# A decoder block's expert stage: a third of the weighted one-hot tiles moved to ScalarE, ten U chunks moved to the dense stage, six chunks' activations kept on chip

## The chip, the cores and the metric

One NeuronCore of a Trainium2 chip runs the whole program. The metric is device time in microseconds (us) of one execution, median of the runs shown. Engine names are those of the profile: PE is the matrix engine, PEld its weight load, DVE the vector engine, ACT the scalar engine, POOL the general engine, SP the engine that issues most DMAs.

## The reference

The program computes one decoder block for 512 tokens of width 1024: attention and gated linear attention, then a product-key expert layer (PEER) and a final norm. Everything the change touches lies in the expert layer. Per token it selects 128 of 16384 experts (8 heads, 16 each) with gates, and computes

```python
ub = jnp.take(u, eb, axis=0)
hid = jax.nn.gelu(jnp.einsum('tkd,td->tk', ub, xb), approximate=False) * gb
vb = jnp.take(v, eb, axis=0)
return jnp.einsum('tk,tkd->td', hid, vb)
```

`u` and `v` are 16384 x 1024 float32, 64 MiB each. `eb` holds the experts of a block of tokens, `gb` their gates.

## The kernel before

**Dense and gathered tokens.** The 512 tokens are four blocks of 128. Blocks 0, 1 and 2 (384 tokens) go the dense way: all experts are multiplied, and the gates of the experts not chosen are zero. Block 3 goes the gathered way: POOL fetches rows of `u` and `v` by index (`fetch_u` and `gather_u`, L1330 and L1340; `gather_v`, L1365 and L1370) and DVE does the dot products and sums. Of the dense blocks, the last 64 tokens get their U products by gathered rows too (`sp_gather` L1278, `sp_dot` L1284: 64 of them, called dots here), so a U product is 128 experts x 320 tokens.

**Chunks.** The experts are 128 chunks of 128, and four chunks `4m`..`4m+3` form one `m`. A chunk's U part is 24 matmuls of 320 columns (`u_matmuls`; `mm3`, L76 to L78, multiplies a high and a low part of each operand); ACT makes the high part of the weights (L69), DVE the low part (L70), and ACT the gelu (`u_gelu`, L965). The V part is 18 matmuls of 512 columns.

**U chunks ahead.** Ninety-six of the 128 U chunks (all even ones, and the odd ones of m = 16 to 31) are computed before the dense stage, list `AHEAD`. Two chunks share one 1 MiB load (`u_load`) and one result tile `ge` of three. When both are done, the ACT queue writes the tile to the DRAM buffer `gsp` (L980).

**The gate stage.** Gates of the dense blocks are made expert by token with one-hot products. For eight tokens (called a half group; two make one of 24 groups, so there are 48) DVE makes a tile `o12` by comparison (`one_hot`, L1178: 128x2048 bf16) one half group in advance, then a weighted tile `o2` (L1196: 128x3072 bf16), which is the second one-hot times the three bf16 parts of the gate. PE does 24 matmuls of 128 columns (L1203), and ACT evicts two PSUM banks (L1205). `o12` has five buffers, shared with other tiles, and `o2` three. The parts of the gate come from `gate_transposes`, `gate_parts` and `gate_rest`. The half groups of block 0 and the first ten of block 1 have two dots each, until the 64 are used up; the last 22 have none. The chunks ahead are placed between these pieces.

**The order of the work.** In this stage the order on DVE and POOL is that of the program (`manual_schedule`), while PE, ACT and SP are ordered by the framework's own timeline. Where the next U chunk goes is decided by two running sums: each piece yields its estimated DVE time and PE time, and a chunk is put in while `p * DVE_ALL < (d + LEAD_U) * PE_ALL`, at 1.14 of DVE and 3.52 of PE. A half group yields 1.14 and 1.68 of DVE and 1.4 of PE.

**The dense stage.** From here on PE, ACT and SP follow the program too. The list `xs` holds the work units: for each `m` one U unit (the two odd chunks, where they were not made ahead) and two V units of two chunks each: 16 U and 64 V units. A unit loads 1 MiB of `u` or `v` into a ring of four tiles (`load_x`, class `Ring`); ACT makes the high part (L1622), DVE the low part (L1631). A V unit also multiplies the stored activations with the gates (L1621) and splits the product (L1625, L1638). The activations come back from `gsp` by `load_pair`, into a ring `pairs` of five tiles: first the three old `ge` tiles, then two new ones. `loads(i)` decides in which order SP issues these loads, and asks for pairs first. Gates come from `Gd`, 1.5 MiB for eight chunks. The 252 remaining row gathers of block 3 are spread over the units by `due`.

Of the kernel before, what the change touches and what calls it, by code (L numbers as in the profile page):

```python
# [7 lines left out]
F32 = mybir.dt.float32  # L8
FR = mybir.dt.float32r
BF = mybir.dt.bfloat16  # L10
I32 = mybir.dt.int32
U32 = mybir.dt.uint32
AF = mybir.ActivationFunctionType
OP = mybir.AluOpType
# [3 lines left out]
P = 128  # L18
# [13 lines left out]
NGRP = TD // TG  # L32
# [4 lines left out]
SB = DENSE[-1]  # L37


ODD_AHEAD = tuple(range(16, 32))  # L40
AHEAD = tuple(c for m in range(P // 4) for c in (4 * m, 4 * m + 2) + ((4 * m + 1, 4 * m + 3) if m in ODD_AHEAD else ()))
RING, RING2 = 3, 2
GR, G2 = 5, 3
TCARGS = dict(schedule_with_timeline_sim=True)
# [3 lines left out]
def peer_block_kernel(ctx: ExitStack, tc: tile.TileContext, a: dict, out: bass.AP):  # L48
# [900 lines left out]
                nc.scalar.activation(h2n[:, half * 512:(half + 1) * 512], pb, AF.Copy)  # L949

    gsp = dr.tile([P // 2, P, 2, TU], F32, name="gsp")
    last_gelu = {}

    def u_load(c):
        u_part.raw[c % 2] = raw([P, 2, KD, P], f"u{c}")
# [8 lines left out]
    def u_gelu(dest, ph):  # L964
        last_gelu["u"] = nc.scalar.activation(dest, ph, AF.Gelu)  # L965

    def u_part(c, lo_eng=None, after=None):

        j = c // 2 % 2
        if j == 0:  # L970
            u_load(c)
            u_part.ge = dnA.tile([P, 2, TU], F32, tag="ge", bufs=RING, name=f"ge{c}")
        with tc.issue_after(gelus[-4].ins) if len(gelus) > 3 and lo_eng is None else nullcontext():
            uh, ul = hilo(u_part.raw[c % 2][:, j], [P, KD, P], f"uc{c}", lo_eng or nc.vector)
        with tc.issue_after(after.ins) if after is not None else nullcontext():
            ph, end = u_matmuls(c, uh, ul)
        u_gelu(u_part.ge[:, j], ph)
        gelus.append(last_gelu["u"])
        if j:
            nc.scalar.dma_start(gsp[c // 2 - 1:c // 2 + 1, :, c % 2, :].rearrange("j p t -> p j t"), u_part.ge)  # L980
        return end

# [137 lines left out]
    def gathered_index():  # L1120
        nc.vector.scalar_tensor_tensor(ix_u, I12[GB][:, 0], 128.0, I12[GB][:, 1], op0=OP.mult, op1=OP.add)
        odd = rt.tile([P, P], I32, name="odd")
        half = rt.tile([P, P], F32, tag="gr3", bufs=1, name="half")
        nc.vector.tensor_copy(odd, I12[GB][:, 1])
        nc.vector.tensor_scalar(odd, odd, 1, None, op0=OP.bitwise_and)
        nc.vector.tensor_copy(half, odd)
        nc.vector.scalar_tensor_tensor(half, half, -63.5, I12[GB][:, 0], op0=OP.mult, op1=OP.add)
        nc.vector.tensor_scalar(half, half, 2.0, None, op0=OP.mult)
        nc.vector.scalar_tensor_tensor(ix_v, I12[GB][:, 1], 128.0, half, op0=OP.mult, op1=OP.add)
        nc.vector.tensor_copy(gg_g, gates[GB])  # L1130
        yield 0.8, 0
# [10 lines left out]
    def gate_transposes(n):  # L1142

        t12 = rt.tile([P, P // 2, 2, 2], BF, tag="t12", bufs=2, name=f"t12{n}")
        for s in range(2):
            pt = bank(f"tr{s}{n}", BK[s])
            tr = nc.tensor.transpose(pt[:, :P], I12[n][:, s], ident)
            nc.scalar.activation(t12[:, :, s], pt[:, :P].rearrange("p (g r) -> p g r", r=2), AF.Copy)
        pt = bank(f"trg{n}", BK[2])
        nc.tensor.transpose(pt[:, :P], gates[n], ident)  # L1150
        gp3 = rt.tile([P, P // 2, 3, 2], BF, tag="gp3", bufs=2, name=f"gp3{n}")
        r = rt.tile([P, P], F32, tag="gr3", bufs=1, name=f"gr3{n}")
        pair = lambda v: v.rearrange("p (g r) -> p g r", r=2)
        nc.scalar.activation(gp3[:, :, 0], pair(pt[:, :P]), AF.Copy)
        trs[n] = t12, gp3, pt, r
        gate_transposes.tr = gate_transposes.tr or tr
        yield 0, 0.6
# [9 lines left out]
    def gate_rest(n):  # L1167
        gp3, pt, r = trs[n][1:]
        pair = lambda v: v.rearrange("p (g r) -> p g r", r=2)
        nc.vector.tensor_tensor(gp3[:, :, 2], pair(r), gp3[:, :, 1], OP.subtract)  # L1170
        yield 0.25, 0

    gate_transposes.tr = None
# [8 lines left out]
        return o12  # L1182

    def gate_group(bi, n, q):
        gp3 = trs[n][1]
        H = TB // 2
        if q % 2 == 0:
            gate_group.gs = rt.tile([P, P // CG, 2, CG, TG], F32, tag="gs", bufs=2, name=f"gs{n}{q}")
        gs = gate_group.gs
        for t0 in range(0, TG, TB):  # L1190
            g0 = (q * TG + t0) // 2
            o12 = gate_group.next or one_hot(n, g0)
            gate_group.next = one_hot(n, g0 + H) if g0 + H < P // 2 else None
            yield 1.14, 0
            o2 = rt.tile([P, H, 3, P, 2], BF, tag="o2", bufs=3, name=f"o2_{n}{q}{t0}")
            nc.vector.tensor_tensor(o2, o12[:, :, 1, None].to_broadcast([P, H, 3, P, 2]),  # L1196
                                    gp3[:, g0:g0 + H, :, None].to_broadcast([P, H, 3, P, 2]), OP.mult)
            for f in range(TB // 4):
                pt = bank(f"pg{n}{q}{t0}{f}", BK[f]).rearrange("p (a b) -> p a b", a=4)
                for i in range(4):  # L1200
                    g, r = divmod(4 * f + i, 2)
                    for m in range(3):
                        nc.tensor.matmul(pt[:, i, :], o12[:, g, 0, :, r], o2[:, g, m, :, r],  # L1203
                                         start=(m == 0), stop=(m == 2))
                evict = nc.scalar.activation(gs[:, :, q % 2, :, t0 + 4 * f:t0 + 4 * f + 4].rearrange("p c i a -> p a c i"),  # L1205
                                             pt.rearrange("p a (c i) -> p a c i", c=P // CG), AF.Copy)
            evicts.append(evict)
            yield 1.68, 1.4
        k = bi * (P // TG) + q
        if bi == len(DENSE) - 1:  # L1210
            nc.scalar.activation(gates_r[0][:, k], gs[:, 0, q % 2], AF.Copy)
        if q % 2:
            writes.append(lambda: (nc.gpsimd if k >= NGRP - 3 else nc.sync).dma_start(
                Gd[:, :, k - 1:k + 1].rearrange("c p g e -> p c (g e)"), gs.rearrange("p c g i t -> p c (g i t)")))
            if k != NGRP - 3:
                writes.pop()()
# [279 lines left out]
    work = chain(route_heads(), *head, woven(0, rows, first_block), woven(1, rows, second_block),  # L1496
                 woven(SB, [], third_block, gate_rest(SB)))
    NL_U = len(AHEAD) - LAST_U
    DVE_ALL = 11 + 4 * 7.6 + 3 + 1.15 * TS + 2.82 * 2 * NGRP + 1.15 * EARLY + 1.14 * (NL_U - WQ_U)
    PE_ALL = 1.4 * 2 * NGRP + 3 + UCOST * (NL_U - WQ_U)  # L1500
    ctx.enter_context(tc.manual_schedule(engines={mybir.EngineType.DVE, mybir.EngineType.Pool}))
    d = p = 0.0
# [60 lines left out]
    one_vraw = lambda name: dn.tile([P, 2, D], F32, tag="vraw", bufs=1, name=name)  # L1563
    old_ge = lambda name: dnA.tile([P, 2, TU], F32, tag="ge", bufs=RING, name=name)
    raws = Ring([one_raw] * 3 + [one_vraw])
    pairs = Ring([old_ge] * RING + [make_ge] * RING2)
    grs = Ring([lambda name: gk.tile([P, NGRP, CG, TG], F32, tag="gring", bufs=1, name=name), make_gr])
    xrest, prest, jrest = list(range(len(xs))), list(range(0, P, 2)), list(range(P // CG))
    src, ge = {}, {}

    def load_x():
        i = xrest.pop(0)
# [6 lines left out]

    def load_pair():  # L1580
        c = prest.pop(0)
        t = ge[c] = pairs.take(f"gp{c}", step["v", c])
        n = 1 if c // 4 in odd_here else 2
        nc.sync.dma_start(t[:, :n], gsp[c // 2, :, :n])

    def load_gates():
        j = jrest[0]
# [25 lines left out]
    def prep(i, extra=()):  # L1613
        k, c = xs[i]
        weigh()
        raw_ = src.pop(i)
        hi, lo = slots[i % 3]
        if k == "v":
            cs = c % CG
            A = gates_r[c // CG][:, :, cs:cs + 2, :]  # L1620
            nc.vector.tensor_tensor(A[:, :NGU], ge.pop(c).rearrange("p j (g t) -> p g j t", g=NGU), A[:, :NGU], OP.mult)  # L1621
        nc.scalar.activation(hi, raw_, AF.Copy)  # L1622
        if k == "v":
            Ah, Al = make_A(f"Ah{c}"), make_A(f"Al{c}")
            nc.scalar.activation(grp(Ah), A, AF.Copy)  # L1625
        before = due[i - 1] if i else EARLY
        if i > 1:
            gather_to((before + due[i] + 1) // 2)
        for piece in extra:
            piece()  # L1630
        nc.vector.tensor_tensor(lo, raw_, hi, OP.subtract)  # L1631
        gather_to(due[i])
        activate()
        if k == "u":
            ready[i] = [(h.rearrange("p (k e) -> p k e", k=KD), l.rearrange("p (k e) -> p k e", k=KD))
                        for h, l in ((hi[:, j], lo[:, j]) for j in range(2))]
        else:
            nc.vector.tensor_tensor(grp(Al), A, grp(Ah), OP.subtract)  # L1638
            ready[i] = [(c + j, Ah[:, j], Al[:, j], hi[:, j], lo[:, j]) for j in range(2)]
        loads(i)  # L1640
# [97 lines left out]
    for i in range(end):  # L1738
# [8 lines left out]
        if k == "u":  # L1747
            for j, halves in enumerate(ready.pop(i)):
                ph = u_matmuls(c + 2 * j, *halves)[0]
                u_gelu(ge[c - 1 + 2 * j][:, 1], ph)  # L1750
                rest_u.discard(c + 2 * j)
        else:
            v_matmuls(ready.pop(i))
# [101 lines left out]
```

## Time and profile before

| | before |
|---|---|
| median of 3 runs | 1484.95 us (1482.62 to 1485.3) |
| the profiled execution, its own time | 1485.28 us |
| its span in the trace | 1483.4 us |
| mean granted PE clock | 0.986 |
| PE busy | 1421.1 us (96%) |
| DVE busy | 1285.1 us (87%) |
| ACT busy | 651.6 us (44%) |
| POOL busy | 609.4 us (41%) |
| DMA moved | 449 MB, mean 303 GB/s |

The time of an execution holds 1.9 us beside the span. Matmuls are pipelined and their ends are modelled, so PE's busy time overstates its work; the count of matmuls in a stretch says how fast it went. The gate stage runs from about 504 us (first half group) to 801 us (its last matmuls), and the dense stage from there to about 1455 us.

### The profile page before, as it was taken

To read this page: it belongs to the slowest core of one execution; us is meant where nothing else is said; L and a number is where in the kernel's file an instruction comes from. 1 tells how busy PE (TensorE), PEld (TensorE's weight loads), DVE (VectorE), ACT (ScalarE), POOL (GpSimd) and SP (SyncE) were. 2 spreads that over 40 slices of the span, in tenths; PEclk is the share of its full clock that TensorE was granted. 3 is DMA by queue.
4 is the path that set the end of the run, shared out by engine and by line. 5 is a ranking of instruction groups with operands and counts; after the bars stand their busy time and mean duration, and the time that the engine had idled before them with its cause. 6 is when DMAs were issued, how large, how long until landed. Compare 5 with 4: busy or idle time off the path is not lost. (4 is left out here: it accounts for less than half of the span.)

```text
span 1483.4 us, 23561 instructions
## 1 busy us (share of the span) xinstructions
PE 1421.1 (96%) x9019; PEld 1257.7 (85%) x9019; DVE 1285.1 (87%) x2305; ACT 651.6 (44%) x918; POOL 609.4 (41%) x401
## 2 busy tenths in 40 slices
PE   5999999999999999999999899999999999999996
PEld 4788787888899989999999778888888887878885
DVE  7777757589999799899997779999999898989996
ACT  4556376533344455555676323333343233233233
POOL 2000000044523444434003558766767665657530
PEclk9999899999999999999999999999999999999998
DMA  9622636344258899998789999999999999999971
GB/s 351 235 86 70 215 92 222 121 180 160 99 196 271 315 344 344 334 339 318 273 273 319 415 413 412 411 412 411 411 413 411 412 404 414 412 404 413 413 300 71
DMA packets 133009, 449.05 MB, mean 303 GB/s; under 512 B 12176, under 2 KB 50336, under 8 KB 112544
## 3 DMA queue, kind: packets, MB, share of 16 engines
q1 hardware_dynamic: 71984, 259.01, 46.4%
q0 software_dynamic: 47136, 171.99, 30.1%
q10 hardware_dynamic: 13776, 16.56, 3.1%
q8 instruction: 70, 1.15, 0.3%
q14 instruction: 43, 0.35, 0.1%
HBM read 402.32 MB, written 45.09 MB: 302 GB/s over the span
## 5 line engine op out<-in xcount | busy, mean ns | idle before, releaser
L76 PE MATMUL ph<-h2Th,his 128*128 128x320 f32 x1024 | 320.6, 313 | 7.1 <-ACT ge L965 7.1
L78 PE MATMUL ph<-h2Th,los 128*128 128x320 f32 x1024 | 315.4, 310 | 1.1 <-DVE los L70 1.1
L77 PE MATMUL ph<-h2Tl,his 128*128 128x320 f32 x1024 | 316.3, 309 | 0.0
L1330 POOL DMA_INDIRECT gu<-in_u_dram,ix_u x128 | 213.3, 1667 | 182.7 <-DVE gu L1340 90.2
L1365 POOL DMA_INDIRECT gv<-in_vP_dram,ix_v x128 | 202.4, 1581 | 101.4 <-DVE gacc L1370 77.2
L76 PEld LDWEIGHTS ph<-h2Th,his 128*128 128x128 f32 x1024 | 193.1, 189 | 9.3 <-ACT ge L965 8.7
L78 PEld LDWEIGHTS ph<-h2Th,los 128*128 128x128 f32 x1024 | 192.5, 188 | 2.0 <-DVE los L70 1.7
L77 PEld LDWEIGHTS ph<-h2Tl,his 128*128 128x128 f32 x1024 | 193.1, 189 | 0.6
L1278 POOL DMA_INDIRECT spr<-in_u_dram,spix x64 | 114.2, 1784 | 172.9 <-DVE spr L1284 130.6
L1340 DVE SCALAR_TENSOR_TENSOR gu<-gu,h2n 128x1024 f32<-128x1024 f32 x128 | 156.1, 1223 | 32.3 <-DMA gu<-in_u_dram,ix_u 32.2
L78 PE MATMUL acc<-his,Al 128*128 128x512 f32 x456 | 178.6, 392 | 4.9 <-DVE Al L1638 4.8
L77 PE MATMUL acc<-los,Ah 128*128 128x512 f32 x456 | 178.2, 391 | 2.4 <-DVE los L1631 2.4
L1625 ACT ACTIVATE Ah<-gr 128x768 fp32r<-128x768 f32 x64 | 54.1, 846 | 284.7 <-DVE gr L1621 163.1
L76 PE MATMUL acc<-his,Ah 128*128 128x512 f32 x456 | 178.0, 390 | 0.0
L1370 DVE SCALAR_TENSOR_TENSOR gacc<-gv,hg,gacc 128x1024 f32<-128x1024 f32 x127 | 162.9, 1282 | 15.3 <-DMA gv<-in_vP_dram,ix_v 15.0
L76 PE MATMUL acc<-hi,Ah 128*128 128x512 f32 x312 | 123.4, 396 | 5.2 <-ACT Ah L1625 5.2
L78 PE MATMUL acc<-hi,Al 128*128 128x512 f32 x312 | 123.8, 397 | 4.3 <-DVE Al L1638 4.2
L77 PE MATMUL acc<-lo,Ah 128*128 128x512 f32 x312 | 123.0, 394 | 1.7 <-DVE lo L1631 1.7
L69 ACT ACTIVATE his<-u 128x1024 fp32r<-128x1024 f32 x96 | 101.2, 1054 | 35.8 <-DMA u<-in_uT_dram 19.0
L70 DVE TENSOR_TENSOR los<-u,his 128x1024 fp32r<-128x1024 f32 x85 | 103.7, 1222 | 9.7 <-ACT his L69 9.7
L78 PEld LDWEIGHTS acc<-his,Al 128*128 128x128 f32 x456 | 85.9, 188 | 25.2 <-DVE Al L1638 7.5
L965 ACT ACTIVATE ge<-ph 128x320 f32<-128x320 f32 x96 | 41.8, 435 | 145.6 <-PE ph L78 142.5
(604 smaller groups left out, 3009.1 us busy)
## 6 DMA issues: line engine op xcount, KB each, us to landing
u<-in_uT_dram SPq DMA_DIRECT2D x48, 1024.0 KB
gr<-Gd SPq DMA_DIRECT2D x15, 1536.0 KB
Gd<-gs SPq DMA_DIRECT2D x10, 2048.0 KB
gsp<-ge ACTq DMA_DIRECT2D x48, 320.0 KB
wa<-in_w_ada_dram SPq DMA_DIRECT2D x12, 1024.0 KB
gp<-gsp SPq DMA_DIRECT2D x32, 320.0 KB
wo<-in_w_out_dram SPq DMA_DIRECT2D x8, 1024.0 KB
wq<-in_wq_dram SPq DMA_DIRECT2D x8, 1024.0 KB
```

Of the source, the lines that this page charges most:

```text
L69: nc.scalar.activation(hi, src, AF.Copy)
L70: lo_eng.tensor_tensor(lo, src, hi, OP.subtract)
L76: nc.tensor.matmul(acc, lh, rh, start=start, stop=False)
L77: nc.tensor.matmul(acc, lh, rl, start=False, stop=False)
L78: return nc.tensor.matmul(acc, ll, rh, start=False, stop=stop)
L965: last_gelu["u"] = nc.scalar.activation(dest, ph, AF.Gelu)
L1278: nc.gpsimd.indirect_dma_start(out=sp[m], out_offset=None, in_=a["u"], in_offset=bass.IndirectOffsetOnAxis(ap=sp["ix", i][:, j:j + 1], axi ...
L1330: nc.gpsimd.indirect_dma_start(out=ur, out_offset=None, in_=a["u"], in_offset=bass.IndirectOffsetOnAxis(ap=ix_u[:, s:s + 1], axis=0))
L1340: nc.vector.scalar_tensor_tensor(ur, ur, 1.0, h2n, op0=OP.mult, op1=OP.mult, accum_out=hid[:, s:s + 1])
L1365: nc.gpsimd.indirect_dma_start(out=vr, out_offset=None, in_=a["vP"], in_offset=bass.IndirectOffsetOnAxis(ap=ix_v[:, s:s + 1], axis=0))
L1370: nc.vector.scalar_tensor_tensor(gacc, vr, hg[:, s:s + 1], gacc, op0=OP.mult, op1=OP.add)
L1625: nc.scalar.activation(grp(Ah), A, AF.Copy)
```

## The change

Four things change.

1. `o2` is made by two engines. DVE multiplies the one-hot by the two higher bf16 parts of the gate (128x2048 instead of 128x3072). The lowest part stays float32 in the tile `r`, and ACT makes that third with one `activation` Copy per token, whose `scale` is a [128, 1] column of `r`: eight instructions of 128x128 for each half group. Input and output are bf16 with a step of two elements. The estimate of the piece goes from 1.68 to 1.2, and in `DVE_ALL` from 2.82 to 2.34.
2. `ODD_AHEAD` starts at m = 21 instead of 16, so ten odd chunks are no longer computed ahead; they become five more U units in the dense stage (21 instead of 16).
3. The even chunks of m = 0, 1 and 2 (six chunks) are now the last ones of `AHEAD`. Their three `ge` tiles are not written to `gsp` and not read back; the V units use them where they are, and the odd chunks of these m put their gelu into a separate tile, so that six V units multiply in two instructions instead of one.
4. The ring `pairs` begins with the two new tiles; the three old ones become free when the V units of m = 0, 1, 2 have used them. Nothing is loaded for the first three m.

```diff
-ODD_AHEAD = tuple(range(16, 32))
-AHEAD = tuple(c for m in range(P // 4) for c in (4 * m, 4 * m + 2) + ((4 * m + 1, 4 * m + 3) if m in ODD_AHEAD else ()))
+ODD_AHEAD = tuple(range(21, 32))
+KEPT = 3
+AHEAD = tuple(c for m in range(KEPT, P // 4) for c in (4 * m, 4 * m + 2) + ((4 * m + 1, 4 * m + 3) if m in ODD_AHEAD else ()))
+AHEAD += tuple(c for m in range(KEPT) for c in (4 * m, 4 * m + 2))
...
-        if j:
+        if c // 4 < KEPT and c % 2 == 0:
+            ge_of[c] = u_part.ge[:, j]
+        elif j:
             nc.scalar.dma_start(gsp[c // 2 - 1:c // 2 + 1, :, c % 2, :].rearrange("j p t -> p j t"), u_part.ge)
...
-        gp3 = rt.tile([P, P // 2, 3, 2], BF, tag="gp3", bufs=2, name=f"gp3{n}")
-        r = rt.tile([P, P], F32, tag="gr3", bufs=1, name=f"gr3{n}")
+        gp3 = rt.tile([P, P // 2, 2, 2], BF, tag="gp3", bufs=2, name=f"gp3{n}")
+        r = rt.tile([P, P], F32, tag="gr3", bufs=2, name=f"gr3{n}")
...
-        nc.vector.tensor_tensor(gp3[:, :, 2], pair(r), gp3[:, :, 1], OP.subtract)
+        nc.vector.tensor_tensor(pair(r), pair(r), gp3[:, :, 1], OP.subtract)
...
-            nc.vector.tensor_tensor(o2, o12[:, :, 1, None].to_broadcast([P, H, 3, P, 2]),
-                                    gp3[:, g0:g0 + H, :, None].to_broadcast([P, H, 3, P, 2]), OP.mult)
+            nc.vector.tensor_tensor(o2[:, :, :2], o12[:, :, 1, None].to_broadcast([P, H, 2, P, 2]),
+                                    gp3[:, g0:g0 + H, :, None].to_broadcast([P, H, 2, P, 2]), OP.mult)
+            for i in range(TB):
+                g, r = divmod(i, 2)
+                nc.scalar.activation(o2[:, g, 2, :, r], o12[:, g, 1, :, r], AF.Copy,
+                                     scale=low[:, 2 * g0 + i:2 * g0 + i + 1])
...
-            yield 1.68, 1.4
+            yield 1.2, 1.4
...
-    pairs = Ring([old_ge] * RING + [make_ge] * RING2)
+    pairs = Ring([make_ge] * RING2 + [old_ge] * RING)
+    pairs.freed = [-1] * (RING2 + RING - KEPT) + [step["v", 4 * m + 2] for m in range(KEPT)]
...
-    xrest, prest, jrest = list(range(len(xs))), list(range(0, P, 2)), list(range(P // CG))
+    xrest, jrest = list(range(len(xs))), list(range(P // CG))
+    prest = [4 * m + 1 for m in range(KEPT)] + list(range(4 * KEPT, P, 2))
...
-        t = ge[c] = pairs.take(f"gp{c}", step["v", c])
-        n = 1 if c // 4 in odd_here else 2
-        nc.sync.dma_start(t[:, :n], gsp[c // 2, :, :n])
+        t = pairs.take(f"gp{c}", step["v", c + 2 * (c % 2)])
+        for j in range(2):
+            ge_of[c + (2 * j if c % 2 else j)] = t[:, j]
+        if c % 2 == 0:
+            ge_of[c, 2] = t
+            n = 1 if c // 4 in odd_here else 2
+            nc.sync.dma_start(t[:, :n], gsp[c // 2, :, :n])
```

More of the change, by code (lines that the diff above doesn't have):

```diff
@@ L951, in peer_block_kernel @@
     gsp = dr.tile([P // 2, P, 2, TU], F32, name="gsp")
-    last_gelu = {}
+    ge_of, last_gelu = {}, {}
     def u_load(c):
@@ L1122, in gathered_index @@
         odd = rt.tile([P, P], I32, name="odd")
-        half = rt.tile([P, P], F32, tag="gr3", bufs=1, name="half")
+        half = rt.tile([P, P], F32, tag="gr3", bufs=2, name="half")
         nc.vector.tensor_copy(odd, I12[GB][:, 1])
@@ L1184, in gate_group @@
     def gate_group(bi, n, q):
-        gp3 = trs[n][1]
+        gp3, _, low = trs[n][1:]
         H = TB // 2
@@ L1498, in peer_block_kernel @@
     NL_U = len(AHEAD) - LAST_U
-    DVE_ALL = 11 + 4 * 7.6 + 3 + 1.15 * TS + 2.82 * 2 * NGRP + 1.15 * EARLY + 1.14 * (NL_U - WQ_U)
+    DVE_ALL = 11 + 4 * 7.6 + 3 + 1.15 * TS + 2.34 * 2 * NGRP + 1.15 * EARLY + 1.14 * (NL_U - WQ_U)
     PE_ALL = 1.4 * 2 * NGRP + 3 + UCOST * (NL_U - WQ_U)
@@ L1565, in peer_block_kernel @@
     raws = Ring([one_raw] * 3 + [one_vraw])
-    pairs = Ring([old_ge] * RING + [make_ge] * RING2)
+    pairs = Ring([make_ge] * RING2 + [old_ge] * RING)
+    pairs.freed = [-1] * (RING2 + RING - KEPT) + [step["v", 4 * m + 2] for m in range(KEPT)]
     grs = Ring([lambda name: gk.tile([P, NGRP, CG, TG], F32, tag="gring", bufs=1, name=name), make_gr])
-    xrest, prest, jrest = list(range(len(xs))), list(range(0, P, 2)), list(range(P // CG))
-    src, ge = {}, {}
+    xrest, jrest = list(range(len(xs))), list(range(P // CG))
+    prest = [4 * m + 1 for m in range(KEPT)] + list(range(4 * KEPT, P, 2))
+    src = {}
     def load_x():
@@ L1620, in prep @@
             A = gates_r[c // CG][:, :, cs:cs + 2, :]
-            nc.vector.tensor_tensor(A[:, :NGU], ge.pop(c).rearrange("p j (g t) -> p g j t", g=NGU), A[:, :NGU], OP.mult)
+            if (c, 2) in ge_of:
+                nc.vector.tensor_tensor(A[:, :NGU], ge_of.pop((c, 2)).rearrange("p j (g t) -> p g j t", g=NGU),
+                                        A[:, :NGU], OP.mult)
+            else:
+                for j in range(2):
+                    nc.vector.tensor_tensor(A[:, :NGU, j], ge_of[c + j].rearrange("p (g t) -> p g t", g=NGU),
+                                            A[:, :NGU, j], OP.mult)
         nc.scalar.activation(hi, raw_, AF.Copy)
@@ L1749, in peer_block_kernel @@
                 ph = u_matmuls(c + 2 * j, *halves)[0]
-                u_gelu(ge[c - 1 + 2 * j][:, 1], ph)
+                u_gelu(ge_of[c + 2 * j], ph)
                 rest_u.discard(c + 2 * j)
```

## The prediction

> **What bounds the kernel now.** I read the windows of the expert stage first, because PE's share over the span (96%) says only that it always has something in flight. The stretches are: 25 half groups with their dots (A), the 22 without dots (B), the passage into the dense stage (C), its part with U units (D), its part with V units alone (E).
>
> ```profile
> core 0: us, PE busy (x) PEld busy (x) DVE busy (x) ACT busy (x) POOL busy (x), PEclk, DMA share, GB/s
> 503.80:715.70 211.90, 203.74 (x1712) 198.91 (x1711) 197.66 (x228) 112.63 (x146) 90.33 (x50) 0.98 0.93 335
> 715.70:799.10 83.40, 82.86 (x875) 80.33 (x874) 77.93 (x74) 60.96 (x83) 7.07 (x5) 1.00 0.79 269
> 799.10:830.00 30.90, 24.87 (x177) 23.40 (x175) 13.93 (x16) 13.81 (x14) 10.27 (x9) 0.94 0.99 370
> 830.00:1165.00 335.00, 332.55 (x1687) 290.87 (x1686) 310.15 (x334) 117.31 (x112) 236.38 (x145) 0.99 1.02 412
> 1165.00:1420.00 255.00, 247.46 (x1083) 202.31 (x1082) 231.69 (x239) 79.69 (x67) 157.40 (x95) 1.00 1.01 408
> ```
>
> PE and DVE are nearly full in A and B. ACT is at 53% in A but already at 73% in B. In D and E the DMA engines are never idle, at 412 GB/s.
>
> To see how much of PE's time is work I price its matmuls at full pace: a stretch of V units alone, one of U chunks alone, and the 24 gate matmuls from their start to that of the next matmul.
>
> ```profile
> 1200.00:1225.00 25.00, 25.00 (x112) 20.71 (x111) 23.83 (x25) 6.90 (x6) 17.06 (x12) 1.00 1.03 412
> 425.00:450.00 25.00, 25.00 (x173) 25.00 (x172) 23.59 (x37) 11.52 (x17) 0.00 (x0) 1.00 0.56 186
> ```
>
> ```profile
> 604.49 1.55 PE L1203 MATMUL pg<-o,o 128*128 128x128 bf16 x24
> 605.85 0.39 PE L76 MATMUL ph<-h2Th,his 128*128 128x320 f32 x1
> ```
>
> So 25/112 = 0.223 us for 512 columns, 25/173 = 0.1445 for 320, and 1.36 us for a half group. A U chunk is 24 x 0.1445 = 3.47 us; a V unit is 36 x 0.223 = 8.04. How many of each lie in A and B, by tile (U products, then gate products), and in D:
>
> ```profile
> 503.80:715.70 211.90, 173.06 (x1109) 165.10 (x1108) 20.09 (x46) 0.98 0.93 335
> 715.70:799.10 83.40, 56.22 (x347) 50.72 (x345) 6.56 (x15) 1.00 0.79 269
> ```
>
> ```profile
> 503.80:715.70 211.90, 38.80 (x600) 50.34 (x50) 0.98 0.93 335
> 715.70:799.10 83.40, 33.94 (x525) 41.90 (x43) 1.00 0.79 269
> ```
>
> ```profile
> 830.00:1165.00 335.00, 236.28 (x1015) 191.75 (x1014) 0.00 (x0) 0.99 1.02 412
> ```
>
> A: 1109 x 0.1445 + 25 x 1.36 = 194 of 211.9 us. B: 50.1 + 29.8 = 80 of 83.4. D: (1687 - 1015) x 0.1445 + 1015 x 0.223 = 324 of 335. E: 1083 x 0.223 = 242 of 255. PE's own work thus fills all but 18, 3, 11 and 13 us of these stretches, and C loses about 8. The change removes no matmul. It can win at most these gaps, some 53 us, and loses wherever it opens new ones. That is the measure for all that follows.
>
> **The change, part by part.**
>
> *The weighted tile.* The rows of A and B together, by engine:
>
> ```profile
> L1196 DVE TENSOR_TENSOR o<-o,gp 128x3072 bf16<-128x3072 bf16 x48 | 84.2, 1755 | 0.1
> L70 DVE TENSOR_TENSOR los<-u,his 128x1024 fp32r<-128x1024 f32 x60 | 73.4, 1223 | 0.0
> L1284 DVE SCALAR_TENSOR_TENSOR spr<-spr,xs 128x1024 f32<-128x1024 f32 x52 | 63.6, 1223 | 14.1 <-DMA spr<-in_u_dram,spix 14.0
> L1178 DVE TENSOR_TENSOR o<-iot,t 128x2048 bf16<-128x2048 bf16 x48 | 58.4, 1222 | 5.4 <-ACT t L1148 3.1 <-PE pg L1203 2.3
> ```
>
> ```profile
> L1205 ACT ACTIVATE gs<-pg 128x512 f32<-128x512 f32 x93 | 93.2, 1110 | 3.0 <-PE pg L1203 3.0
> L69 ACT ACTIVATE his<-u 128x1024 fp32r<-128x1024 f32 x59 | 62.2, 1054 | 19.0 <-DMA u<-in_uT_dram 19.0
> L965 ACT ACTIVATE ge<-ph 128x320 f32<-128x320 f32 x61 | 26.6, 437 | 100.0 <-PE ph L78 96.9 <-issue 3.2
> ```
>
> On DVE the piece shrinks from 1755 ns to what 128x2048 bf16 takes, 1222 (L1178): 0.53 us saved per half group. On ACT eight instructions come in. No row has bf16 in and out with a step and a scale column; the nearest has the shape and the scale column, in f32:
>
> ```profile
> 16.32 0.70 ACT L497 ACTIVATE Eg<-ident,ra1y 128x128 f32<-128x128 f32 x2 [2.79 <-POOL ra1y L94]
> ```
>
> ```profile
> 790.66 0.34 ACT L1211 ACTIVATE gr<-gs 128x128 f32<-128x128 f32 x1
> 790.87 1.11 ACT L1205 ACTIVATE gs<-pg 128x512 f32<-128x512 f32 x1
> ```
>
> The two L497 take 0.70 together and a single one 0.40 (its group's mean is 396 ns), so each after the first adds 0.30. Without a scale column the next instruction starts 0.21 after a 128x128 copy. Bounds for one token: 0.21 (scale column free) and 0.40 (no overlap at all). I take 0.30, the row of the same form: 8 x 0.30 = 2.4 us for each half group, four and a half times what DVE saves.
>
> *Ten chunks fewer ahead.* By the two running sums, worked through with the kernel's constants, A gets 40 chunks where these sums gave 45, and B 9 where they gave 14. Each takes 3.47 us of PE, 1.14 of DVE (what L70 adds in a row of others) and about 1.3 of ACT (L69 and L965, less their overlap of 0.1 each) out of the gate stage.
>
> *A after.* DVE: 197.7 - 25 x 0.53 - 5 x 1.14 = 179, plus its 14 us of waits for gathered rows: 193. PE: 194 - 17 = 177, plus 18 of gaps: 195. ACT: 112.6 + 25 x 2.4 - 5 x 1.3 = 166, below both. So A shrinks by 18 at best. But at 86% ACT makes its queue felt: the high part of the next chunk stands behind eight tokens, and DVE's low part and PE wait for it. Bounds -18 and -5; I take **-15**.
>
> *B after.* DVE: 77.9 - 22 x 0.53 - 5 x 1.14 = 61. PE: 80 - 17 = 63. ACT: 61.0 + 22 x 2.4 - 5 x 1.3 = **107**, and B lasted 83.4. ACT becomes the bound by a wide margin. `o2` has three buffers and `o12` is made one half group ahead, so ACT cannot do this work earlier, in A, where it has room; and the chunks that could fill PE are tied to DVE's order. Behind the tokens on ACT stand the evictions, the high parts and the gelus, and for these wait PE and then DVE. With 4 us of waits that remain: 111, **+28**. Bounds from the token's price: at 0.21 B takes 91.5 and 4 (+12, or +8 without the 4), at 0.40 it takes 125 and 4 (+46).
>
> *The dense stage.* Ten chunks are 34.7 us more of PE work there, 5 MiB more of `u` loads, and less traffic with `gsp`.
>
> ```profile
> u<-in_uT_dram SPq DMA_DIRECT2D x48, 1024.0 KB
> gr<-Gd SPq DMA_DIRECT2D x15, 1536.0 KB
> ...
> gp<-gsp SPq DMA_DIRECT2D x32, 320.0 KB
> ...
> gp<-gsp SPq DMA_DIRECT2D x32, 160.0 KB
> ```
>
> ```profile
> L1370 DVE SCALAR_TENSOR_TENSOR gacc<-gv,hg,gacc 128x1024 f32<-128x1024 f32 x118 | 151.3, 1283 | 15.2 <-DMA gv<-in_vP_dram,ix_v 15.0
> L1340 DVE SCALAR_TENSOR_TENSOR gu<-gu,h2n 128x1024 f32<-128x1024 f32 x124 | 151.3, 1223 | 31.4 <-DMA gu<-in_u_dram,ix_u 31.4
> ```
>
> A gathered row tile is 128x1024 f32, 0.524 MB. `due` spreads 252 of them by the weights 1.63 (U chunk pair) and 1.37 (V), which gives 3.24 for each V unit of E now. Such a unit moves 1.049 + 0.393 (a quarter of a gate load) + 0.328 + 3.24 x 0.524 = 3.47 MB: at 412 GB/s that is 8.42 us, against 8.04 on PE. The trace has 255 us for 1083/36 = 30.1 units, 8.47 each. So E is held by DMA. An `m` of D (one U, two V units, 3.87 and 3.24 gathers) moves 9.69 MB, 23.5 us, against 6.94 + 16.07 = 23.0 on PE; the trace has 23.8. With five more U units the shares fall to 3.59 and 3.01 gathers: the V unit of E to 3.35 MB, 8.13 us; the `m` of D to 9.30 MB, 22.6 us, so that PE's 23.0 holds. Before: 16 x 23.5 + 32 x 8.42 = 645. After: 21 x 23.0 + 22 x 8.13 = 662, **+17**. The split multiplication in six V units adds below 0.1 us each by L1621's 821 ns for 640 columns, on a DVE that is busy 310 of 335 us; uncovered it would be 0.5 us.
>
> *The passage (C).* SP, ACT and PE here:
>
> ```profile
> 794.97 17.94 SPq L1584 DMA_DIRECT2D gp<-gsp  x3
> 812.96 0.96 SPq L1578 DMA_DIRECT2D v__8740<-in_vP_dram  x1
> ```
>
> ```profile
> 824.24 1.91 ACT L1622 ACTIVATE hi<-v__8740 128x2048 fp32r<-128x2048 f32 x1 [9.03 <-DMA v__8740<-in_vP_dram]
> ```
>
> The third load of activations goes into an old `ge` tile that is still to be written out, and SP stands at it until 812.96, with the first V load behind it. That load lands at 824 and PE has run dry. After the change no load stands there for the first three `m`; the V load can go when its own buffer is free, which the last low part (L70 at 799.16) decides, some 12 us earlier. PE has U units to do until about 818, so its gap closes: I take **-6** of C's 8 (bounds -8 and 0). What is late next is the gathers that the full DMA queues delay.
>
> *The rest.* `gate_rest` writes f32 instead of bf16, three instructions of 0.3 us: nothing. Three writes and six reads of `gsp` less: in the DMA sums above.
>
> **Sum.** -15 + 28 + 17 - 6 = +24, on the profiled execution's 1485.3 us (span 1483.4): **1509 us**. That execution lies 0.3 us above the median.
>
> **The rivals.**
>
> *ACT's order and a cold PE (1539).* If ACT evicts a half group right after its tokens, it waits for the 1.55 us of gate matmuls each time: 22 x 1.55 = 34 more, B at 141, sum +54. For it: L1205 already waits for PE now and then (3.0 us). A slow PE gives the same sign:
>
> ```profile
> 550.00:553.00 3.00, 1.12 (x20) 0.94 (x17) 2.81 (x4) 0.20 (x1) 1.68 (x1) 1.00 1.04 425
> 553.00:556.00 3.00, 1.76 (x6) 1.77 (x7) 2.33 (x3) 3.00 (x5) 0.83 (x1) 0.52 0.99 402
> 556.00:560.00 4.00, 4.00 (x17) 4.00 (x17) 4.00 (x6) 1.01 (x2) 3.06 (x2) 0.50 0.62 200
> ```
>
> After about 3 us without matmuls the granted clock falls to half for some 7 us. A half group of B without a chunk would leave PE idle for 4.9 - 1.36 = 3.5 us. The Trainium skill (TensorE: Matmul & The Clock Gate, part 1, the HAM clock gate) puts the limit at an idle window of about 3.4 us; by it the gaps of B lie right at the edge. Against: DVE is ahead, so the next half group's tokens can go before the eviction.
>
> *The other side: a cheap token (1477).* If ACT passes bf16 twice as fast and hides the scale column (0.05 + 0.10 = 0.15 us), B is 54.5 + 176 x 0.15 = 81, A gains its 18, and the sum is -18 - 2 + 17 - 6 = -9. It decides below 0.18 us a token, where B stays under 87 us. For it: DVE passes 2048 bf16 in the time of 1024 f32 (L1178 and L1284). Against: the 0.21 of L1211. The Trainium skill (ScalarE: Activation LUTs, What ACT_TABLE_LOAD costs) gives bf16 the pace of fp32, and 186 + 93 ns + 0.833 ns per element less 93 ns of overlap. By it a token is an estimated 0.29 us and this rival falls. Its Rules for kernel authors would leave multiplications on VectorE.
>
> *The dense stage gives nothing back (1533).* If the gaps of C to E come from landing times and not from the mean rate, all 34.7 us are paid: -15 + 28 + 35 = +48. For it: DVE's 31.4 and 15.0 us of waits for gathered rows. Against: E's 8.47 us a unit meets the DMA sum.
>
> **How the numbers follow.** Forecast 0.60, with its own range 1495 to 1525; order and cold clock 0.15; dense stage 0.14; cheap token 0.11. This kernel's runs tell no change within 0.2% (3 us). Faster is the cheap token: 0.11. Same is the forecast's far edge: 0.02. Slower: 0.87. The range reaches from B at 0.21 a token (1485 - 15 + 8 + 17 - 6 = 1489) to a little above the second rival: 1490 to 1548.
>
> **What would show it.** Right: ACT above 95% in B and B near 111 us; PE there with gaps that end on ACT, and about 40 us emptier than before; A near 197; the first V load issued near 801 and no gap of PE in C; V units of E at 8.1 us. Wrong: tokens spaced below 0.2 us, or B still ended by DVE; then the forecast is too high by 20 us or more.

## The result and the profile after

The changed kernel takes 1502.09 us (median of 4 runs, 1498.61 to 1504.54) against 1483.83 for the kernel before: ratio 1.0121, 95% interval [1.0097, 1.0145]. It is slower by 18 us. The forecast was 1509, with 1490 to 1548 as its range. The profiled execution took 1501.71 us with a span of 1499.9, 16.5 more than the span before.

The windows of the changed kernel, cut at matching marks (start of the first one-hot, start of the 27th weighted tile, and the end of the last weighted tile, which is now the end of ACT's last token):

```profile
core 0: us, PE busy (x) PEld busy (x) DVE busy (x) ACT busy (x) POOL busy (x), PEclk, DMA share, GB/s
499.60:700.90 201.30, 185.47 (x1569) 181.02 (x1569) 177.12 (x222) 161.43 (x349) 83.30 (x50) 0.97 0.91 328
700.90:800.80 99.90, 84.40 (x802) 76.38 (x802) 64.61 (x73) 98.69 (x244) 5.69 (x5) 0.91 0.64 215
800.80:830.00 29.20, 25.58 (x160) 24.12 (x158) 17.14 (x18) 16.89 (x20) 16.13 (x11) 0.94 1.01 398
830.00:1270.00 440.00, 440.00 (x2261) 386.59 (x2260) 406.01 (x431) 151.90 (x143) 311.43 (x183) 1.00 1.02 406
1270.00:1440.00 170.00, 170.00 (x752) 140.72 (x751) 153.90 (x154) 55.73 (x46) 90.02 (x59) 1.00 1.00 400
```

In the second row, the half groups without dots, ACT is busy 98.69 of 99.90 us, where it was 60.96 of 83.40. PE has 15.5 us without any matmul there and DVE 35. In the two dense rows PE is busy in every microsecond, where it was not before.

ACT's groups in the gate stage, and its timeline inside B:

```profile
L1204 ACT ACTIVATE o<-o,gr 128x128 bf16<-128x128 bf16 x384 | 124.3, 444 | 5.8 <-DVE o L1182 5.8
L1213 ACT ACTIVATE gs<-pg 128x512 f32<-128x512 f32 x93 | 96.4, 1089 | 0.8 <-PE pg L1211 0.8
```

```profile
734.75 4.28 ACT L1204 ACTIVATE o<-o,gr 128x128 bf16<-128x128 bf16 x14
738.85 0.46 ACT L967 ACTIVATE ge<-ph 128x320 f32<-128x320 f32 x1
739.16 0.47 ACT L1204 ACTIVATE o<-o,gr 128x128 bf16<-128x128 bf16 x1
739.46 1.10 ACT L1213 ACTIVATE gs<-pg 128x512 f32<-128x512 f32 x1
...
743.77 1.08 ACT L1213 ACTIVATE gs<-pg 128x512 f32<-128x512 f32 x1
744.62 1.60 ACT L1204 ACTIVATE o<-o,gr 128x128 bf16<-128x128 bf16 x5
```

One token lasts 444 ns, but 14 in a row take 4.28 us: (4.28 - 0.44)/13 = 0.295 each. In B, ACT is idle for 1.2 us in all; what waits is on the other engines (the two rows of POOL have their like in the kernel before, 71.2 and 10.6 us):

```profile
POOL gu L1338 <- PE pg L1211: 82.3, 2, 78.1
POOL Gd L1221 <- DVE gu L1348: 16.7, 1, 16.7
DVE los L72 <- ACT his L71: 12.6, 3, 9.8
...
DVE o L1200 <- PE pg L1211: 7.5, 5, 2.9
PE pg L1211 <- ACT gs L1213: 7.2, 12, 2.4
```

DVE stands 12.6 us at the high part of the next U chunk, which is queued on ACT behind tokens, and PE 7.2 us for PSUM banks that ACT has not evicted.

At the entry to the dense stage SP no longer stands. Its timeline after:

```profile
787.42 0.33 SPq L1586 DMA_DIRECT2D u__8809<-in_uT_dram  x1
797.94 0.33 SPq L1588 DMA_DIRECT2D v__8817<-in_vP_dram  x1
802.00 0.33 SPq L1588 DMA_DIRECT2D v__8819<-in_vP_dram  x1
```

The first V load goes 3 us before the gate stage ends; before the change it went 12 us after.

PE's gap at this place closed only in part, though. These are the 30 us after the last weighted tile, in the kernel before, in the changed kernel, and in the run below that has the kept chunks and the ring order alone:

```profile
799.20:829.20 30.00, 24.05 (x173) 22.79 (x170) 13.03 (x13) 13.00 (x14) 10.27 (x9) 0.95 0.99 369
800.80:830.80 30.00, 26.38 (x163) 24.80 (x161) 17.94 (x20) 16.89 (x20) 16.48 (x12) 0.94 1.01 398
798.50:828.50 30.00, 29.33 (x201) 27.75 (x199) 18.00 (x22) 16.69 (x18) 13.29 (x11) 1.00 1.02 406
```

In the changed kernel PE waits for the high and the low part of the first U unit of the dense stage:

```profile
807.40 0.41 PE L78 MATMUL ph<-h2Th,his 128*128 128x320 f32 x1 [1.85 <-ACT his L1642]
...
809.72 0.42 PE L80 MATMUL ph<-h2Th,los 128*128 128x320 f32 x1 [1.77 <-DVE los L1651]
```

The kernels below with 86 and 90 chunks ahead and the whole tile on DVE have the same two waits (1.9 and 1.8 us); those with 92 and 96 and the new ring order have not. So they go with the number of chunks ahead and not with the tokens; why is open.

One part of the 16.5 us is not the change's. DVE's instructions up to the first half group come in the same order, yet the changed kernel's profile has it 4.2 us earlier. Between 100 and 200 us the clock differs (before, then after):

```profile
100.00:150.00 50.00, 49.77 (x555) 43.02 (x553) 35.39 (x94) 27.93 (x66) 1.26 (x1) 0.93 0.24 85
150.00:200.00 50.00, 47.98 (x403) 39.46 (x403) 36.90 (x89) 22.76 (x72) 0.00 (x0) 0.90 0.51 167
```

```profile
100.00:150.00 50.00, 48.77 (x538) 41.85 (x539) 37.42 (x97) 27.66 (x65) 1.27 (x1) 1.00 0.25 87
150.00:200.00 50.00, 47.13 (x441) 39.64 (x437) 37.32 (x98) 28.89 (x87) 0.00 (x0) 1.00 0.46 148
```

The 0.93 and 0.90 are means over 50 us. In steps of 4 us the kernel before has 1.00 there except for two falls to about half, of which these are the lowest rows; the changed kernel has 1.00 throughout:

```profile
112.00:116.00 4.00, 4.00 (x65) 3.24 (x67) 3.24 (x10) 2.09 (x10) 0.00 (x0) 0.60 0.02 4
116.00:120.00 4.00, 4.00 (x24) 3.67 (x20) 2.93 (x13) 3.19 (x1) 0.00 (x0) 0.54 0.00 0
...
168.00:172.00 4.00, 4.00 (x56) 2.86 (x58) 3.97 (x10) 0.60 (x1) 0.00 (x0) 0.50 0.81 262
172.00:176.00 4.00, 4.00 (x51) 3.54 (x47) 3.79 (x11) 1.42 (x4) 0.00 (x0) 0.50 0.77 227
```

By DVE's instructions the changed kernel is 1.8 us ahead at 100 us, 3.9 after the first fall, 7.0 after the second, and 4.2 at the first half group. So single profiles differ by several microseconds from one execution to the next, and below, medians carry the verdicts and profiles only say where the time went.

### The profile page after: what moved, and what is told of

The parts are those of the page before. It is cut to its first block, busy times and chain, and to the rows that moved or that the text cites. A ratio compares the mean times of both kernels' runs of the same rounds, so it can differ in the third digit from the quotient of the medians.

```text
span 1499.9 us, 23906 instructions
## 1 busy us (share of the span) xinstructions
PE 1426.9 (95%) x9019; PEld 1263.2 (84%) x9019; DVE 1260.9 (84%) x2306; ACT 749.9 (50%) x1297; POOL 606.4 (40%) x401
## 4 chain that ended last, share of the span: by engine, by line
PE 69%; DVE 9%; ACT 9%; DMA 5%; issue 4%; POOL 3%; ACTq 0%; POOLq 0%; SPq 0%; DVEq 0%
PE acc L80 12%; PE acc L78 11%; PE acc L79 11%; PE ph L78 7%; PE ph L80 7%; PE ph L79 6%; POOL spr L1286 3%; ACT o L1204 3%; ACT gs L1213 2%; DMA spr<-in_u_dram,spix 2%; DMA wa<-in_w_ada_dram 1%; DVE macc L240 1%; PE pj L474 1%; DMA u<-in_uT_dram 1%; DVE los L72 1%
## 5 line engine op out<-in xcount | busy, mean ns | idle before, releaser
L1286 POOL DMA_INDIRECT spr<-in_u_dram,spix x64 | 105.5, 1648 | 173.0 <-DVE spr L1292 127.1
L79 PE MATMUL acc<-los,Ah 128*128 128x512 f32 x432 | 169.2, 392 | 2.4 <-DVE los L1651 2.4
L80 PE MATMUL acc<-his,Al 128*128 128x512 f32 x432 | 169.2, 392 | 0.1
L78 PE MATMUL acc<-his,Ah 128*128 128x512 f32 x432 | 168.8, 391 | 0.0
L78 PE MATMUL acc<-hi,Ah 128*128 128x512 f32 x336 | 131.6, 392 | 0.0
L79 PE MATMUL acc<-lo,Ah 128*128 128x512 f32 x336 | 130.9, 390 | 0.0
L1204 ACT ACTIVATE o<-o,gr 128x128 bf16<-128x128 bf16 x384 | 124.3, 444 | 5.8 <-DVE o L1182 5.8
L72 DVE TENSOR_TENSOR los<-u,his 128x1024 fp32r<-128x1024 f32 x75 | 91.3, 1218 | 25.3 <-ACT his L71 25.3
L71 ACT ACTIVATE his<-u 128x1024 fp32r<-128x1024 f32 x86 | 90.7, 1057 | 30.9 <-DMA u<-in_uT_dram 14.1
L1292 DVE SCALAR_TENSOR_TENSOR spr<-spr,xs 128x1024 f32<-128x1024 f32 x64 | 77.9, 1219 | 29.6 <-DMA spr<-in_u_dram,spix 29.3
```

The costliest lines, as they stand in the source:

```text
L71: nc.scalar.activation(hi, src, AF.Copy)
L72: lo_eng.tensor_tensor(lo, src, hi, OP.subtract)
L78: nc.tensor.matmul(acc, lh, rh, start=start, stop=False)
L79: nc.tensor.matmul(acc, lh, rl, start=False, stop=False)
L80: return nc.tensor.matmul(acc, ll, rh, start=False, stop=stop)
L1204: nc.scalar.activation(o2[:, g, 2, :, r], o12[:, g, 1, :, r], AF.Copy, scale=low[:, 2 * g0 + i:2 * g0 + i + 1])
```

## The experiments

Every run's median, and the stages of its profiled execution: A from the first one-hot to the 27th weighted tile, B from there to the start of the last gate matmul, the rest from there to the end of the span.

| kernel | median | A | B | rest |
|---|---|---|---|---|
| before | 1483 to 1487 | 211.9 | 85.3 | 682.4 |
| the change | 1502.1 | 201.3 | 100.8 | 698.2 |
| tokens alone (96 ahead) | 1504.6 | 207.6 | 104.1 | 683.0 |
| chunks and kept, no tokens (86) | 1486.7 | 208.9 | 77.8 | 701.1 |
| kept and ring order alone (96) | 1476.2 | 213.8 | 85.1 | 673.1 |
| the change, tokens only with dots (86) | 1486.3 | 200.6 | 81.2 | 699.0 |
| the change, tokens without scale column | 1488.0 | 201.0 | 86.1 | 701.6 |
| ring order alone (96) | 1482.4 | 214.9 | 85.4 | 678.2 |
| kept, 100 ahead | 1480.7 | 217.8 | 88.1 | 668.5 |
| kept, 92 ahead | 1469.9 | 204.5 | 82.9 | 678.6 |
| kept, 92 ahead, again | 1468.7 | 205.8 | 81.8 | 678.6 |
| kept, 90 ahead | 1473.5 | 206.0 | 80.6 | 686.6 |
| the change, 92 ahead | 1491.8 | 206.4 | 104.5 | 676.3 |

The theory was the forecast's: ACT's tokens bind the half groups without dots, the entry to the dense stage gains, and the moved chunks cost a part of their PE time. The rival was that the moved chunks are what costs.

**One part at a time.** Tokens alone, with their estimates for placing the chunks, on the kernel before:

```diff
-            nc.vector.tensor_tensor(o2, ... [P, H, 3, P, 2] ...)
+            nc.vector.tensor_tensor(o2[:, :, :2], ... [P, H, 2, P, 2] ...)
+            for i in range(TB):
+                nc.scalar.activation(o2[:, g, 2, :, r], o12[:, g, 1, :, r], AF.Copy, scale=low[...])
```

> The kernel before with the token instructions on ACT alone; 96 chunks ahead, nothing kept. Theory (ACT's tokens bind the 22 half groups without dots): no change in the dense stage, A about 10 us shorter, B from 83 to about 106 us (61 of ACT work and 44 to 46 of tokens, ACT at 98% or more): about 1496 us (1490 to 1502). Rival (the ten chunks moved to the dense stage are what costs, the tokens are harmless or help): 1484 or less.

Measured: 1504.63 us, ratio 1.0154 [1.0113, 1.0194]. B, up to 812:

```profile
710.20:812.00 101.80, 88.95 (x852) 81.91 (x851) 65.82 (x74) 101.00 (x245) 6.94 (x5) 0.93 0.64 220
```

ACT is busy 101.00 of 101.80 us. The median lies above the expected 1490 to 1502. The tokens alone cost as much as the whole change, within the intervals; the rival's 1484 is out. A fell by 4 instead of 10 us.

The changed kernel with the whole weighted tile on DVE:

```diff
-            nc.vector.tensor_tensor(o2[:, :, :2], ...)
-            for i in range(TB): nc.scalar.activation(...)
+            nc.vector.tensor_tensor(o2, ... [P, H, 3, P, 2] ...)
```

> The changed kernel with the whole weighted tile on DVE again; 86 chunks ahead and six kept. Theory: A about 10 us shorter and B some 10 to 14 us shorter (fewer chunks, ACT no bound), dense stage 15 longer: about 1476 us (1470 to 1484). Rival (the moved chunks cost): about 1499.

Measured: 1486.70 us, ratio 1.0015 [0.9995, 1.0034]. Both theories missed. B fell by 7.5, but A by 3, and the rest grew by 18.7 where 15 was expected. So tokens cost 1502.1 - 1486.7 = 15 us, and the other parts together nothing that these runs can tell.

Kept chunks and the new ring order alone, on the kernel before:

```diff
-ODD_AHEAD = tuple(range(21, 32))
+ODD_AHEAD = tuple(range(16, 32))
```

(The edit is shown against the kernel of the run just described. Against the kernel before, parts 3 and 4 of the change are left.)

> The kernel before with the six kept chunks and the new order of the pair ring alone. Theory: PE's gap at the entry to the dense stage goes, 6 to 8 us: about 1478 us (1474 to 1484). Rival (the gap only moves to the next wait for DMA, since DMA holds the dense stage anyway): 1484, no change.

Measured: 1476.24 us, ratio 0.9952 [0.9934, 0.9970]: faster. The rest fell by 9.3 us, of which 5.3 is PE's gap at the entry (29.33 us busy in the first 30, where it was 24.05). So the ten moved chunks cost 1486.7 - 1476.2 = 10.5 us in the medians.

Tokens only where there are dots; the last 22 half groups get the third part from a second DVE instruction:

```diff
+            on_act = bi * (P // TB) + g0 * 2 // TB < ON_ACT  # 26
+            if not on_act:
+                nc.vector.tensor_tensor(o2[:, :, 2], o12[:, :, 1], thirds[n][...], OP.mult)
-            for i in range(TB):
+            for i in range(TB if on_act else 0):
```

> The changed kernel with ACT's tokens only in the 26 half groups that have dots; in the last 22 DVE makes all three parts, in two instructions. Theory: A stays 10 us shorter, B falls from 100 to about 72 us and is bound by DVE again, dense stage as in the changed kernel: about 1474 us (1466 to 1482), faster than both. Rival (tokens cost wherever they are, or the moved chunks cost): 1495 or more.

Measured: 1486.32 us, ratio 1.0012 [0.9992, 1.0031]. B falls to 81.2, so the cost of the tokens does sit in the last 22. But the expected gain in A does not reach the median: it equals that of the kernel without tokens (1486.7), although its profile has A 8 us shorter and B 3 longer. That profile is one of the fastest of ten executions, 3.9 us under their median. What the second DVE instruction and run-to-run differences take of it stays open.

**The price of a token.** The scale column is dropped, nothing else; the third part is then the bare one-hot:

```diff
-                nc.scalar.activation(o2[:, g, 2, :, r], o12[:, g, 1, :, r], AF.Copy, scale=low[...])
+                nc.scalar.activation(o2[:, g, 2, :, r], o12[:, g, 1, :, r], AF.Copy)
```

> The changed kernel whose tokens are plain copies without a scale column; the third part of the weighted tile is then the bare one-hot, so the gates come out as other numbers. Everything else is as in the changed kernel. Theory (ACT's instructions bind the half groups without dots): each of some 170 tokens there is 0.085 us shorter, B falls by 14 us, A by at most 3: about 1487 us (1483 to 1494). Rival (B waits for PE, evictions or DVE, and ACT is only busy along with it): 1498 or more.

Measured: 1487.98 us, 14 less than the change. B and a row of tokens:

```profile
707.30:793.00 85.70, 72.14 (x778) 67.95 (x777) 64.39 (x73) 83.29 (x238) 5.54 (x5) 0.96 0.68 233
```

```profile
736.57 3.35 ACT L1204 ACTIVATE o<-o 128x128 bf16<-128x128 bf16 x16
```

Sixteen tokens take 3.35 us, (3.35 - 0.40)/15 = 0.197 each, 0.098 less than with the column. B fell by 14.7 us, from 100.8 to 86.1, and 170 x 0.098 is 16.7. ACT still binds at 83.29 of 85.70 us. B follows the price of one ACT instruction, as the theory says. (This profile is the slowest of ten executions, mainly because its first half group comes 6.7 us later than the change's, with the same work up to there; the length of B does not hang on that.)

**The entry to the dense stage.** The kernel before with the pair ring turned round, all traffic as before:

```diff
-    pairs = Ring([old_ge] * RING + [make_ge] * RING2)
+    pairs = Ring([make_ge] * RING2 + [old_ge] * RING)
```

> The kernel before with the two new tiles first in the pair ring, nothing else: activations are still written out and read back. Theory (SP standing at the load into a tile not yet written out is what costs at the entry to the dense stage): most of what the kept chunks gave, about 1478 us (1474 to 1481). Rival (the saved traffic of six chunks gives it): 1483 to 1487.

Measured: 1482.38 us, ratio 0.9968 [0.9950, 0.9986], between the two. SP's timeline:

```profile
802.03 1.78 SPq L1584 DMA_DIRECT2D gp<-gsp  x3
803.91 0.41 SPq L1578 DMA_DIRECT2D v__8740<-in_vP_dram  x1
```

SP stands 1.8 instead of 17.9 us and the V load goes at 803.9 instead of 813.0. The first 30 us after the last weighted tile:

```profile
801.10:831.10 30.00, 29.02 (x200) 27.46 (x197) 19.29 (x21) 16.87 (x18) 14.53 (x11) 1.00 1.02 408
```

So the order alone closes PE's gap. The rest falls by 4.2 us; with the kept chunks it falls by 9.3, but the two medians (ratios 0.9968 and 0.9952, with intervals that overlap) do not separate them. What not loading the first activations adds is not shown.

**How many chunks ahead.** Kept chunks, whole tile on DVE, `ODD_AHEAD` from 14, 18 and 19:

```diff
-ODD_AHEAD = tuple(range(16, 32))
+ODD_AHEAD = tuple(range(14, 32))   # then 18, and 19
```

> Kept chunks and the new ring order, whole tile on DVE, 100 chunks ahead instead of 96. Theory (the dense stage is held by DMA more than by PE, so chunks taken out of it give back only their bytes, while the gate stage pays PE in full): about 1480 us (1476 to 1486). Rival (PE bounds both stages, a chunk costs the same in either): 1476.

> The same with 92 chunks ahead. By the two runs with 96 and 86 (1476 and 1487) each chunk moved to the dense stage costs about 1 us: about 1480 us (1476 to 1484). Rival (the best split lies between 86 and 96): 1472 to 1475.

> Kept chunks and ring order, whole tile on DVE, 90 chunks ahead. Theory (the dense stage is bound by PE from 92 downwards): two chunks cost their full 7 us there and the gate stage gives back at most 2: about 1475 us (1471 to 1479). Rival (the best split lies lower still): 1469 or less.

> The kernel with 92 ahead once more, beside the two others on one chip: 1470 us (1467 to 1474).

Measured: 1480.71 with 100, 1469.93 with 92 (ratio 0.9874 [0.9836, 0.9911]), 1473.51 with 90, and 1468.71 with 92 again (0.9884 [0.9851, 0.9917]). The expectation for 92 was wrong; its rival (1472 to 1475) had the direction, and the run fell lower still: a straight line between 96 and 86 hid a kink. The other three came within their ranges. The dense stage, from 30 us after its start to 30 before the end, with 96, 92 and 86:

```profile
828.50:1443.40 614.90, 605.39 (x2890) 513.45 (x2890) 568.98 (x599) 205.84 (x187) 404.11 (x243) 1.00 1.00 401
```

```profile
818.80:1439.30 620.50, 617.49 (x2993) 528.20 (x2992) 572.38 (x601) 212.28 (x195) 398.05 (x243) 1.00 1.00 400
```

```profile
811.60:1454.60 643.00, 643.00 (x3165) 554.91 (x3164) 583.26 (x608) 220.84 (x206) 407.81 (x244) 1.00 0.98 389
```

With 96, DMA is never idle and PE misses 9.5 us. With 92 both are full. With 86 PE is busy all 643 us and DMA has room. So from 96 to 92 the rest grows by 5.5 us for 13.9 us of PE work (four chunks at 3.47), and from 92 to 86 by 22.5 for 20.8.

The gate stage bends at the same place: A and B together take 305.9 us with 100 chunks ahead, 298.9 with 96, 287.4 with 92, 286.6 with 90 and 286.7 with 86. DVE's work and its waits for gathered rows fill A with 96, 92 and 86 alike, and what moves most between them is these waits (from 500 to 705 us, with 96, 92 and 86):

```profile
DVE spr L1288 <- DMA spr<-in_u_dram,spix: 15.7, 10, 3.8
DVE spr L1288 <- DMA spr<-in_u_dram,spix: 9.3, 13, 1.8
DVE spr L1288 <- DMA spr<-in_u_dram,spix: 16.8, 13, 3.2
```

In the second run with 92 they are 10.6 us in A. Why they are shortest there is open, so a part of what 92 gains is not explained. The kernel with 92 beats both kernels of the case.

**The change with 92 ahead.**

```diff
-ODD_AHEAD = tuple(range(21, 32))
+ODD_AHEAD = tuple(range(18, 32))
```

> The changed kernel with 92 chunks ahead instead of 86 (odd ones from m = 18). Theory (two separate costs: ACT's tokens bind the half groups without dots, and below 92 chunks ahead PE bounds the dense stage): the dense stage falls by some 20 us as it does without tokens, the gate stage grows by 6 to 10 us since ACT has six more chunks to serve: about 1490 us (1484 to 1496), still 15 to 20 above the same kernel without tokens. Rival (the tokens cost only because of the many chunks moved): 1470 to 1475.

Measured: 1491.76 us, ratio 1.0054 [1.0031, 1.0076], as expected: rest 22 us shorter than in the change, B 4 longer, and 22 to 23 us above the same kernel without tokens. So both costs are there at once, but they do not simply add: six more chunks ahead gain 17 us without tokens (1486.7 to 1469.9) and 10 with them (1502.1 to 1491.8), where A is 5 us longer too.

## Why the prediction was right, and where its terms were off

The sign, the place and the cause hold: ACT above 95% in B, PE emptier there, and B's length moving with the price of a token. The sum was 24, measured 18 in the medians and 16.5 in the profiles, 20.7 if one counts from the first half group on. Of the forecast's signs, three did not come as stated: B near 111 us, C without a gap of PE, and PE 40 us emptier in B. By the forecast's prices PE has 260 x 0.1445 + 539 x 1.36/24 = 68 us of work in the 99.9 us of B, so it is 28 us emptier than before.

- **A token's price** (0.30) was right: 0.295. The rival of a cheap token falls with it (its sum of -9 gives 1476, not 1477). By the Trainium skill (ScalarE: Activation LUTs, What ACT_TABLE_LOAD costs) it would be an estimated 0.29 with the scale column and 0.20 without. The traces have 0.295 and 0.197, so here, for bf16 with a step, the page agrees on the pace.
- **B** (+28) was too high: +15.5, or +16.5 by the forecast's own cut. The step that failed is "ACT 61.0 + 52.8 - 6.5 = 107, and 4 us of waits". ACT's busy time came to 98.7. Counted from each start to the next, the 170 tokens of B took 48.9 us (0.288 each; the sum had 176 at 0.30), and ACT's other work 49.8 instead of 54.5. That work was charged at what it takes on an ACT that is often idle: an eviction lasts 1.1 us, but when the next instruction is ready it starts 0.85 us after it (743.77 and 744.62 above), where in the kernel before it took 0.96 on average. And ACT waited 1.2 us, not 4.
- **The rival of ACT's order** (1539) did not happen: ACT's evictions waited 0.8 us for PE in the whole gate stage. The mean clock did fall to 0.91 in B, but PE still stood without a matmul for 15.5 us there.
- **A** (-15) was -10.6 in the profile. The step that failed is "plus its 14 us of waits for gathered rows": as DVE's work shrinks, it seems to come to the rows only earlier. Its waits there grew from 14.0 to 20.9 us, and it waited another 3.0 for a high part behind tokens:

```profile
L1292 DVE SCALAR_TENSOR_TENSOR spr<-spr,xs 128x1024 f32<-128x1024 f32 x52 | 63.3, 1218 | 21.0 <-DMA spr<-in_u_dram,spix 20.9
```

  In all five kernels with tokens in A these waits are 20.9 to 25.4 us, in the eight without tokens 9.0 to 21.8.
- **The entry** (-6): that the third load of activations holds SP was right, and the V load went as early as forecast. But PE was busy only 2.3 us more of the first 30 (26.38 for 24.05). The step that failed is "PE has U units to do until about 818, so its gap closes": PE waited 1.85 and 1.77 us for the parts of the first of these units. With 96 chunks ahead the step holds.
- **The ten chunks in the dense stage** (+17) were about right, by the forecast's own units. The V part in D:

```profile
830.00:1270.00 440.00, 309.36 (x1349) 252.09 (x1348) 0.00 (x0) 1.00 1.02 406
```

  These are 37.5 V units, beside 912 U matmuls or 19 U units: 23.4 us for an `m` (forecast 23.0), and 170/(752/36) = 8.14 for a V unit of E (8.13). So 21 x 23.4 + 22 x 8.14 = 670, where the kernel before has 16 x 23.8 + 32 x 8.47 = 652: some +19. With the entry's 2.3 off, that is near the 15.8 by which the rest grew. Against a kernel whose gap at the entry is closed the ten chunks cost more: +28.0 between the profiles with 96 and 86. PE misses only 9.5 us there in the long stretch, and the gap opens again. From 92 downwards each chunk is paid in full. The rival "the dense stage gives nothing back" is thus nearer for the last six chunks than the forecast.

The errors have opposite signs: B 12.5 too high, A 4.4 and the two last terms together 4.8 too low (15.8 for 11). The sum was better than its terms, and that is luck. The 4.2 us before the first half group had no term; they are a difference between two executions.

## What to carry to other kernels

An engine that is at 44% over the span can be at 73% in the one stage that gets new work: price added work against the busiest stage it falls in, and per instruction, since eight short ACT instructions at 0.295 us replaced 0.53 us of DVE. Work moved into a stage held by DMA costs less than its PE time until PE is full there too (5.5 us for 13.9 here), and its full price beyond that (22.5 for 20.8), so two points do not give a slope. When a change has several parts, run them one at a time: here kept chunks and ring order gained 7 to 9 us and 92 chunks ahead another 6 to 8, under tokens that cost 15 to 23.

## What was not expected of the hardware

A 128x128 bf16 copy on ACT lasts 444 ns with a scale column and 401 without, yet follows its predecessor after 295 and 197 ns. The duration of one says little of the pace of many. In one profile of an unchanged stretch PE's granted clock fell twice to about half, for some 7 and 10 us; in another it stayed at 1.00, and that execution gained 5 us on the first there. A mean of 0.9 over 50 us hides such falls. What set them off is open: in the 12 us before the first, PE was busy in every row.
